# Seven block products instead of eight in the last blocks of four jobs, and operand halves issued two per step there

## The chip, the cores and the metric

The kernel runs on one core of a Trainium2 chip. The metric is the device time of one execution in microseconds (us). The engines are named as in the profile: PE (TensorE, matmuls), PEld (its weight loads), DVE (VectorE), ACT (ScalarE), POOL (GpSimd) and SP (SyncE, which issues nearly all DMAs here).

## What is computed

One layer of a streaming encoder in fp32 on 2048 tokens of width 1024: token mixing (sliding-window attention beside a gated recurrence), cross-attention into 256 memory tokens, and a SwiGLU feed-forward, each inside RMS norms. The change lies in the feed-forward:

```
u = rms_norm(h, g_ffn_pre[l])
y = (jax.nn.silu(u @ w_gate[l]) * (u @ w_up[l])) @ w_down[l]
h = h + rms_norm(y, g_ffn_post[l])
```

`w_gate` and `w_up` are 1024 x 2816, `w_down` is 2816 x 1024.

## The kernel before

**Products.** A fp32 operand is split into a rounded part and a remainder (hi and lo, `split2`, line 982: hi by a copy on ACT or POOL, lo by a subtraction on DVE), and each product of 128 x 128 by 128 x 512 is three matmuls: hi hi, hi lo, lo hi (`products`, lines 1122 to 1124).

**Blocks.** From the output projection on, all large products go through `phases` (line 1210). A block is a 2 x 2 scheme: the moving operand T (resident, four quarters of nk x 128 rows by 512 columns) times the stationary operand S (streamed, 256 columns). There are two ways to do a block:

- seven products (kind "s", `seven`, line 1126), by combinations of the quarters. It uses the resident operands 1, 5, 6, 3, 7, 2, 4 in that order; 1, 2 and 3 are plain quarters, 5, 6, 7 and 4 are sums and differences of them. The stream gives 7 splits and 4 combinations on DVE (`streamed`, line 1063), three first parts are copied off PSUM by ACT (line 1137), and three of the four outputs are additions on DVE.
- eight products (kind "p", `eight`, line 1166) by the plain quarters 1, 2, 8, 3, with 4 stream splits and no combination. It takes two products in each of its 4 steps; a seven-product block takes one in each of its 7.

**Jobs.** `jobs` (line 1411) lists them in order: output projection, scores, values, the feed-forward half 0 and half 1 (each 1024 tokens of u as T, 22 blocks that alternate gate and up over the hidden columns), and three chunks of the down product (8 blocks each, w_down as T; nk is 3 in the first, 4 in the others). `kinds` (line 1423) makes every block "s" and the last one of a job "p"; the very last block of the last job is set back to "s" by hand. In the output projection the first block is "p" too.

**Resident operands.** Seven buffers hold T operands (four of one pool, three of another, line 1227). A queue of operands, in order of first use, is fed by `half` (line 1262): when the buffer with the earliest last use is free at the present step, half an operand is taken up: its DMA into a "row" buffer (nine of them) is issued by SP, and its split into hi and lo is put on a list, due two steps later. `split` (line 1253) takes one due entry off that list, an ACT copy and a DVE subtraction for each half. Sums for 5, 6, 7 and 4 have been made earlier and lie in DRAM (`u0_s`, `u_s`, `d_s`). If an operand is asked for and not there yet, `Ready` (line 1288) issues what is missing at once.

**The order.** The main loop (lines 1331 to 1360) goes through the steps. After a step's matmuls are traced it makes the stream operands two steps ahead (`upto`), advances the work that trails a block (`after`), and calls `split` and `half` once in a step of a seven-product block, twice in a step of an eight-product block. A split that is due is queued behind the step's last ACT and DVE instructions (`behind`, line 1048). The tile framework's scheduler then orders the traced instructions of each engine; after that, each engine runs its list in order.

**Outputs near the change.** Gate blocks end in a Silu on ACT, up blocks in a product on DVE and a store of the hidden rows by SP (line 78). A down block's rows are stored to `y2_d` (shown as `y_d`); from the second chunk on, POOL first adds what is there by an accumulating DMA (line 1500), and SP's store waits for it.

Of the kernel before, what the change touches and what calls it, by code (L numbers as in the profile page):

```python
# [25 lines left out]
NFF = DFF // P  # L26
# [3 lines left out]
NT = T // P  # L30
# [18 lines left out]
class Layer:  # L49
# [89 lines left out]
    def split(self, raw, hi, lo, engine="P"):  # L139

        self.split2(raw, hi, lo, engine)
# [52 lines left out]
    def mix(self):  # L194
        tc, I = self.tc, self.I
        kw = dict(reuse_waits="tile")
        with contextlib.ExitStack() as left:
# [43 lines left out]
            with tc.tile_pool(name="xp", bufs=1, side="right", **kw) as self.xp:  # L241
                fold = self.fold_cross()
                for _ in range(2):
                    next(fold)
                for i, _ in enumerate(pairs, 1):
                    for _ in range(2):
                        next(fold)
                    if 2 <= i < 10:
                        next(phases)
                for _ in fold:  # L250
                    pass
# [199 lines left out]
    def in_first(self):  # L451
# [83 lines left out]
        phases = self.phases([(lambda i, j, a, n: raw[i, j][:, a:a + n, :], 4, blocks, None, {})], T)  # L535
        PE, ACT, DVE, POOL = (getattr(mybir.EngineType, e) for e in ("PE", "Activation", "DVE", "Pool"))
        next(phases)
        self.turns("h", 36)
        x_loads(1, (0, 1))
# [6 lines left out]
        with self.queued(self.traced(POOL), self.traced(DVE)):  # L546
            next(phases)
# [623 lines left out]
    def plain(self, S, T, nk, out, keep, kind):  # L1171
# [36 lines left out]
        yield  # L1208

    def phases(self, jobs, first, prologue=None):  # L1210


# [18 lines left out]
        if first:  # L1231
            for i, p in enumerate(first):
                k = (0, p, False)
# [5 lines left out]
        def fetch(n, tile):  # L1239
            def get(i, j, a, c):  # L1240
                t = tile().rearrange("p (k d) -> p k d", d=512)[:, :c]
                if j is None:
                    self.load(t.rearrange("p k d -> p (k d)"), jobs[n][3][self.CHAIN.index(i), :, a * 512:(a + c) * 512])
                else:
                    jobs[n][0](t, i, j, a, c)
                return t

            return jobs[n][0] if first else get

        def lag(k):  # L1250
            return 2 if k[1] in self.BLOCK or jobs[k[0]][3] is not None else 0

        def split(g):

            if pending and pending[0][0] <= g:
                _, k, f = pending.pop(0)
                f()
                left[k] -= 1
                return True
            return False  # L1260

        def half(g, tile):

            if current[0] is None:
                if not queue:
                    return False
                free = min(slots, key=lambda s: s[1])
                if free[1] > g:
                    return False
                n, p, _ = k = queue.pop(0)  # L1270
                slots.remove(free)
                slots.append((free[0], uses[k][-1], free[2]))
                self._n += 1
                dst = (self.big if free[0] == "A" else self.tb).tile(
                    [P, 2, 4, 512], F32R, tag="big" if free[0] == "A" else "T", name=f"T_{self._n}",
                    bufs=4 if free[0] == "A" else 3)[:, :, :jobs[n][1]]
                T[k] = dst
                left[k] = 2
                current[:] = [(k, self.resident(fetch(n, tile), jobs[n][1], p, dst, keep[n], jobs[n][3] is not None)), 0]
            k, f = current[0]  # L1280
            pending.append((g + lag(k), k, next(f)))
            current[1] += 1
            if current[1] == 2:
                next(f, None)
                current[0] = None
            return True
# [13 lines left out]
        blocks = [b for job in jobs for b in job[2]]  # L1300
        streams, ready, made = [], [], [0]

        def stream(at):
            if at < len(blocks):
                streams.append(blocks[at][1](blocks[at][0]))
                next(streams[-1])

        def upto(count):
            while made[0] < count:
                s = next(streams[0], None)  # L1310
                if s is None:
                    streams.pop(0)
                    continue
                ready.append(s)
                made[0] += 1
# [12 lines left out]
        g = 0  # L1328
        at = 0
        self.last = {}  # L1330
        for _, nk, bl, _, beside in jobs:
            for i, (kind, _, out, follow, addend) in enumerate(bl):
                stream(at + 1)
                after += [f() for f in beside.get(i, ())]
                run = (self.seven(ready, Ready(), nk, out, addend) if kind == "s" else
                       self.eight(ready, Ready(), nk, out) if kind == "p" else
                       self.plain(ready, Ready(), nk, out, addend, kind))
                for q in range(len(self.STEPS[kind])):
                    for _ in range(1 if g or not first else 3):
                        next(run)  # L1340
                        if first and g < 3:
                            yield
                    self.mark()
                    upto(need[g + 2])
                    if first and g == 1:
                        yield
                    for _ in range(1 if kind == "s" else 2):
                        for f in list(after):
                            if next(f, after) is after:
                                after.remove(f)  # L1350
                        if pending and lag(pending[0][1]):
                            with self.behind():
                                split(g)
                        else:
                            split(g)
                        if not first or g > 1:
                            half(g, self.row_tile)
                    g += 1
                after.append(follow())
                at += 1  # L1360
        for f in after:
            for _ in f:
# [48 lines left out]
    def jobs(self):  # L1411
        I = self.I

        def weights(src, r0, nk):
            return lambda t, i, j, k0, n: self.load(
                t, src[r0 + (i * nk + k0) * P:r0 + (i * nk + k0 + n) * P, j * 512:(j + 1) * 512]
                .rearrange("(k p) d -> p k d", p=P))

        def ffn_u(b):
            return lambda t, i, j, k0, n: self.load(  # L1420
                t, self.u_d[4 * i + k0:4 * i + k0 + n, :, b * TB + j * 512:b * TB + (j + 1) * 512]
                .rearrange("k p t -> p k t"))

        def kinds(blocks, n=0):
            return [("p" if i < n or i == len(blocks) - 1 else "s",) + b for i, b in enumerate(blocks)]

        def sums(name, src, nk, other=None):
            return self.sums(name, src, nk, self.extra_tile, other or self.gain_tile)

        def in_turn(*what):  # L1430
            return lambda: itertools.chain.from_iterable(w() for w in what)

        qk, vo = weights(self.qk_d, 0, 4), weights(self.vo_d, 0, 4)
        down = [(weights(I["w_down"], f0 * P, nk), f0, nk) for f0, nk in ((0, 3), (6, 4), (14, 4))]
        qk_s, vo_s = sums("qk_s", qk, 4, self.row_tile), sums("vo_s", vo, 4)
        u_s = sums("u_s", ffn_u(1), 4)
        self.u0_s = self.tc.dram_tile([4, P, 4 * 512], F32, name="u0_s")
        d_s = [sums(f"d_s{c}", src, nk) for c, (src, _, nk) in enumerate(down)]
        jobs = [(self.w_out, 4, kinds([self.mixed_block(n) for n in range(0, NT, 2)], 1), self.out_sums, {1: [qk_s[1]]}),
                (qk, 4, kinds([self.score_block(n) for n in range(0, NT, 2)]), qk_s[0], {1: [vo_s[1]]}),  # L1440
                (vo, 4, kinds([self.value_block(n) for n in range(0, NT, 2)]), vo_s[0], {})]
        for b in range(NB):
            beside = {2: [in_turn(*(d[1] for d in d_s))]} if b else {4: [u_s[1]]}
            jobs.append((ffn_u(b), 4, kinds([blk for f in range(0, NFF, 2) for blk in self.hidden_blocks(b, f)]),
                         u_s[0] if b else self.u0_s, beside))
        for c, (src, f0, nk) in enumerate(down):
            jobs.append((src, nk, kinds([self.down_block(c, f0, nk, n) for n in range(0, NT, 2)]), d_s[c][0], {}))
        k, s, o, f, a = jobs[-1][2][-1]
        jobs[-1][2][-1] = ("s", s, o, f, a)

        return jobs

# [302 lines left out]
```

## Time and profile before

| | |
|---|---|
| time, median of 3 runs | 2589.82 us (2588.64 to 2592.41) |
| span of the profiled execution | 2585.7 us |
| median less that span | 4.1 us |
| busy: PE, PEld, DVE, ACT, POOL | 99%, 83%, 68%, 49%, 17% |
| matmuls and transposes on PE | 12371 |
| DMA | 506.03 MB, mean 196 GB/s |

Only the span is given for the profiled execution; what lies around it is taken to be the 4.1 us between it and the median. A row of the groups names the line, the engine, the operation, what it writes and reads with the shapes, how often, the busy time and the mean of one, and after the bar the engine's idle time just before these instructions with what ended it. In the windows view each engine's busy time and number of instructions stand for a stretch of time, with the granted PE clock, the busy share of the DMA engines and their rate. In the timeline a row gives start, length, engine, line, operation and how many were merged. T is a resident operand, S a stream operand, `psm` a PSUM bank, `sraw` the raw stream, `row` a row buffer, `part` a first part copied off PSUM.

### The profile page before, as it was taken

The page shows a single profiled execution, that of the slowest core. Times are in us where ns is not written, and L with a number is a line of the kernel's source. Part 1 is how long each engine was busy: PE and PEld are TensorE (multiplying, and loading weights), DVE is VectorE, ACT ScalarE, POOL GpSimd, SP SyncE. Part 2 cuts the span into 40 slices and gives each one's busy share as a digit, 9 for nine tenths or more (in the row PEclk, how much of TensorE's full clock was granted, in tenths as well). Part 3 has the DMA queues.
Part 4 walks back from the last instruction along what each step waited for, and adds up shares of the span by engine and source line. Part 5 has one row for each costly group of instructions (what it writes and reads, how often), then busy time and mean ns, then how long its engine had stood idle before and what let it go on. Part 6 is the DMA issues. An engine that isn't in the chain of part 4 may idle for free.

```text
span 2585.7 us, 34998 instructions
## 1 busy us (share of the span) xinstructions
PE 2548.3 (99%) x12371; PEld 2135.9 (83%) x12371; DVE 1747.9 (68%) x2759; ACT 1261.0 (49%) x2633; POOL 428.4 (17%) x612
## 2 busy tenths in 40 slices
PE   9999999999999999999999999999999999999998
PEld 8888888888988778888878888888888888888886
DVE  7785588986557778788876655576566556564656
ACT  5563466665555566465563333353333334443543
POOL 5231334321302232222300000000000000000022
PEclk9999999999999999999999999999999999999999
DMA  6445655855888886666963622253565444566888
GB/s 188 147 163 179 198 168 152 253 185 167 258 290 281 296 287 210 205 222 210 327 233 115 203 97 75 98 203 124 177 205 194 146 146 139 208 201 186 262 213 218
DMA packets 363663, 506.03 MB, mean 196 GB/s; under 512 B 20960, under 2 KB 249312, under 8 KB 363488
## 3 DMA queue, kind: packets, MB, share of 16 engines
q1 hardware_dynamic: 357440, 481.77, 56.5%
q0 software_dynamic: 6048, 22.02, 4.7%
q8 instruction: 97, 1.59, 0.2%
q14 instruction: 78, 0.64, 0.1%
HBM read 337.00 MB, written 166.72 MB: 195 GB/s over the span
## 4 chain that ended last, share of the span: by engine, by line
PE 83%; DMA 7%; DVE 4%; ACT 3%; issue 2%; POOL 1%; SPq 0%; DVEq 0%; POOLq 0%; ACTq 0%
PE psm L1122 23%; PE psm L1124 23%; PE psm L1123 22%; PE psg L156 2%; PE psg L157 2%; PE psg L158 2%; PE pss L1374 1%; DMA row<-y_d 1%; DMA raw<-in_wo_x_dram 1%; DMA u_d<-row 1%; DMA h1t_d<-row 1%; DMA row<-h_d 1%; ACT junk L1471 1%; ACT T L985 0%; PE pss L837 0%
## 5 line engine op out<-in xcount | busy, mean ns | idle before, releaser
L1122 PE MATMUL psm<-T,S 128*128 128x512 f32 x2695 | 1043.8, 391 | 11.0 <-ACT part L1137 6.5
L1123 PE MATMUL psm<-T,S 128*128 128x512 f32 x2695 | 1049.1, 390 | 2.1 <-DVE T L988 1.9
L1124 PE MATMUL psm<-T,S 128*128 128x512 f32 x2695 | 1038.9, 390 | 3.6 <-DVE S L988 3.6
L1122 PEld LDWEIGHTS psm<-T,S 128*128 128x128 f32 x2695 | 506.2, 188 | 120.3 <-ACT part L1137 7.0
L1124 PEld LDWEIGHTS psm<-T,S 128*128 128x128 f32 x2695 | 506.2, 188 | 110.4 <-DVE S L988 5.3
L1123 PEld LDWEIGHTS psm<-T,S 128*128 128x128 f32 x2695 | 506.5, 188 | 107.5 <-DVE T L988 4.1
L985 ACT ACTIVATE S<-sum 128x512 fp32r<-128x512 f32 (+1 forms) x314 | 188.7, 619 | 359.6 <-PE psm L1124 267.8
L988 DVE TENSOR_TENSOR S<-sraw,S 128x512 fp32r<-128x512 f32 (+1 forms) x319 | 217.0, 687 | 215.9 <-ACT S L985 201.8
L988 DVE TENSOR_TENSOR S<-sum,S 128x512 fp32r<-128x512 f32 (+1 forms) x372 | 249.7, 681 | 47.0 <-ACT S L985 31.8
L1137 ACT ACTIVATE part<-psm 128x512 f32<-128x512 f32 x273 | 161.7, 597 | 242.8 <-PE psm L1124 221.5
L985 ACT ACTIVATE S<-sraw 128x512 fp32r<-128x512 f32 (+1 forms) x272 | 167.4, 617 | 111.2 <-PE psm L1124 99.3
L1500 POOL DMA_DIRECT2D row<-y_d x28 | 25.7, 919 | 1111.4 <-DVE row L1686 1036.5
L988 DVE TENSOR_TENSOR T<-row,T 128x1024 fp32r<-128x1024 f32 (+1 forms) x120 | 141.3, 1192 | 60.9 <-ACT T L985 60.4
L1471 ACT ACTIVATE junk<-row 128x512 f32<-128x512 f32 x160 | 99.7, 625 | 60.5 <-DVE row L1493 30.0
L157 PE MATMUL psg<-u,whi 128*128 128x512 f32 x320 | 127.8, 399 | 0.0
L158 PE MATMUL psg<-u,wlo 128*128 128x512 f32 x320 | 127.1, 397 | 0.0
L156 PE MATMUL psg<-u,whi 128*128 128x512 f32 x320 | 127.1, 397 | 0.0
L985 ACT ACTIVATE T<-row 128x1024 fp32r<-128x1024 f32 x120 | 119.9, 1028 | 10.5 <-DMA row<-qk_s 3.5
L987 POOL TENSOR_SCALAR S<-sum 128x512 fp32r<-128x512 f32 x58 | 53.4, 921 | 294.6 <-PE psm L1124 237.2
L1637 DVE TENSOR_TENSOR row<-psm,part 128x512 f32<-128x512 f32 x66 | 43.7, 687 | 61.4 <-PE psm L1124 61.3
L1646 DVE TENSOR_TENSOR part<-psm,part 128x512 f32<-128x512 f32 x60 | 39.7, 687 | 62.4 <-PE psm L1124 62.2
L812 ACT ACTIVATE S<-S,w_mn 128x256 f32<-128x256 f32 (+1 forms) x128 | 63.1, 495 | 28.6 <-DVE w_mn L808 28.3
(363 smaller groups left out, 3679.1 us busy)
## 6 DMA issues: line engine op xcount, KB each, us to landing
sraw<-in_w_gate_dram SPq DMA_DIRECT2D x44, 512.0 KB, 3.7
sraw<-in_w_up_dram SPq DMA_DIRECT2D x44, 512.0 KB, 3.7
hid_d<-row SPq DMA_DIRECT2D x44, 512.0 KB, 2.7
h_d<-row SPq DMA_DIRECT2D x32, 512.0 KB, 4.8
y_d<-row SPq DMA_DIRECT2D x32, 512.0 KB, 3.3
sraw<-hid_d SPq DMA_DIRECT2D x32, 512.0 KB, 5.1
row<-y_d POOLq DMA_DIRECT2D x28, 512.0 KB, 7.1
sraw<-in_w_in_dram SPq DMA_DIRECT2D x44, 256.0 KB, 3.5
```

Of the source, the lines that this page charges most:

```text
L156: nc.tensor.matmul(ps, ah, bh, start=(i == 0), stop=False)
L157: nc.tensor.matmul(ps, ah, bl, start=False, stop=False)
L158: nc.tensor.matmul(ps, al, bh, start=False, stop=(i == n - 1))
L812: nc.scalar.activation(s[:, r, o:], s[:, r, o:], AF.Exp, bias=mn[:, i:i + 1], scale=-1.0, accum_out=den[:, i:i + 1])
L985: self.nc.scalar.activation(hi, raw, AF.Copy)
L987: self.nc.gpsimd.tensor_scalar(hi, raw, 1.0, 1.0, ALU.mult, ALU.mult)
L988: self.nc.vector.tensor_tensor(lo, raw, f32(hi), ALU.subtract)
L1122: nc.tensor.matmul(ps, s[:, 0, k, :], t[:, 0, k, :], start=st, stop=False, **kw)
L1123: nc.tensor.matmul(ps, s[:, 0, k, :], t[:, 1, k, :], start=False, stop=False, **kw)
L1124: nc.tensor.matmul(ps, s[:, 1, k, :], t[:, 0, k, :], start=False, stop=sp, **kw)
L1137: nc.scalar.activation(t, ps, AF.Copy)
L1471: self.nc.scalar.activation(junk, a, AF.Square, scale=float(D) ** -0.5, accum_out=to)
```

## The change

The last block of the two feed-forward halves and of the first two down chunks becomes a seven-product block. In that block two splits may be taken per step and, after its first, fourth and seventh step, a second half; in the block after it, two splits per step. The other jobs (output projection, scores, values) keep their eight-product last block.

```
+        fresh = False
         for _, nk, bl, _, beside in jobs:
             for i, (kind, _, out, follow, addend) in enumerate(bl):
...
+                change = kind == "s" and i == len(bl) - 1
                 for q in range(len(self.STEPS[kind])):
...
                     for _ in range(1 if kind == "s" else 2):
...
                         if not first or g > 1:
                             half(g, self.row_tile)
+                    if change or kind == "s" and fresh:
+                        split(g)
+                        if change and q in (0, 3, 6):
+                            half(g, self.row_tile)
                     g += 1
                 after.append(follow())
+                fresh = change
                 at += 1
...
-        def kinds(blocks, n=0):
-            return [("p" if i < n or i == len(blocks) - 1 else "s",) + b for i, b in enumerate(blocks)]
+        def kinds(blocks, n=0, last="p"):
+            return [("p" if i < n else last if i == len(blocks) - 1 else "s",) + b for i, b in enumerate(blocks)]
...
-            jobs.append((ffn_u(b), 4, kinds([blk for f in range(0, NFF, 2) for blk in self.hidden_blocks(b, f)]),
+            jobs.append((ffn_u(b), 4, kinds([blk for f in range(0, NFF, 2) for blk in self.hidden_blocks(b, f)], 0, "s"),
                          u_s[0] if b else self.u0_s, beside))
         for c, (src, f0, nk) in enumerate(down):
-            jobs.append((src, nk, kinds([self.down_block(c, f0, nk, n) for n in range(0, NT, 2)]), d_s[c][0], {}))
-        k, s, o, f, a = jobs[-1][2][-1]
-        jobs[-1][2][-1] = ("s", s, o, f, a)
+            jobs.append((src, nk, kinds([self.down_block(c, f0, nk, n) for n in range(0, NT, 2)], 0, "s"), d_s[c][0], {}))
```

The extra `split` is not put behind the step's last instructions, as the one in the loop above it is.

## Prediction

> **What bounds the kernel now.** I read the page first: the busy times, then the chain that ended last.
>
> ```profile
> span 2585.7 us, 34998 instructions
> ...
> PE 2548.3 (99%) x12371; PEld 2135.9 (83%) x12371; DVE 1747.9 (68%) x2759; ACT 1261.0 (49%) x2633; POOL 428.4 (17%) x612
> ...
> PE 83%; DMA 7%; DVE 4%; ACT 3%; issue 2%; POOL 1%; SPq 0%; DVEq 0%; POOLq 0%; ACTq 0%
> ```
>
> PE is busy nearly all the time and makes up most of the chain, so a removed matmul is worth something only if PE finds its next operand ready. The stretch that the change touches is then read by groups of instructions (PE alone, the idle time before each group in the last column), and as one window.
>
> ```profile
> L1123 PE MATMUL psm<-T,S 128*128 128x512 f32 x1702 | 661.1, 389 | 0.0
> L1124 PE MATMUL psm<-T,S 128*128 128x512 f32 x1702 | 654.4, 389 | 0.0
> L1122 PE MATMUL psm<-T,S 128*128 128x512 f32 x1702 | 653.5, 389 | 0.0
> ...
> core 0: us, PE busy (x) PEld busy (x) DVE busy (x) ACT busy (x) POOL busy (x), PEclk, DMA share, GB/s
> 1342.00:2499.00 1157.00, 1157.00 (x5106) 958.01 (x5106) 692.44 (x1013) 462.61 (x796) 26.28 (x35) 1.00 0.52 165
> ```
>
> From 1342 to 2499 us PE never waits: 5106 matmuls in 1157.00 us, one every 1157.00 / 5106 = 0.2266 us (389 ns is the length of one, overlapped). All four changes that the diff touches lie in it. So PE alone bounds this stretch, and I have to ask two things: how many matmuls go, and what waits appear in their place.
>
> **The change part by part.** An eight-product block runs 8 x nk x 3 matmuls, a seven-product block 7 x nk x 3. Three of the four blocks have nk 4 (12 fewer each), the first down chunk has nk 3 (9 fewer): 45, which is also the difference of the two built programs' PE lists. 45 x 0.2266 = **10.2 us** off PE if nothing waits. That is certain as work.
>
> The other lists of the built programs differ by 32 more on DVE, 10 more on ACT, 8 fewer on SP, none on POOL. Per block DVE gains 3 stream splits, 4 combinations and 3 additions of outputs and loses the two splits of operand 8; SP loses that operand's two loads. PE's third PSUM bank per block comes from a pool of six; I cost it at nothing, since seven-product blocks run back to back without a wait in the rows above (if a bank were late, PE would wait one DVE output, 0.6 us below).
>
> The extra calls of split and half do no work of their own; they move operand loads and splits. Before, the eight-product block needed operands 1, 2, 8, 3 only, so the buffers of 5, 6, 7 and 4 were free a block early. Now all seven are used to the end, the next job's operand p can be written only after the last block's product p, and it is needed seven products later. Fourteen halves, each one ACT copy and one DVE subtraction, must pass in about two blocks. That is the price to work out. DVE and ACT at the present changes (first and second, third and fourth row are one change each, the last two rows are the changes of the down chunks):
>
> ```profile
> 1692.00:1730.00 38.00, 38.00 (x169) 31.46 (x168) 26.04 (x33) 19.68 (x27) 0.00 (x0) 1.00 0.73 262
> 1730.00:1768.00 38.00, 38.00 (x170) 31.45 (x169) 28.85 (x40) 20.14 (x31) 0.00 (x0) 1.00 0.28 88
> 2114.00:2150.00 36.00, 36.00 (x161) 29.80 (x160) 21.61 (x32) 16.62 (x27) 0.00 (x0) 1.00 0.62 219
> 2150.00:2164.00 14.00, 14.00 (x64) 11.58 (x63) 12.53 (x19) 9.24 (x16) 0.00 (x0) 1.00 0.26 85
> 2240.00:2275.00 35.00, 35.00 (x156) 28.97 (x155) 25.65 (x34) 21.25 (x34) 0.00 (x0) 1.00 0.93 328
> 2403.00:2441.00 38.00, 38.00 (x170) 31.45 (x169) 26.20 (x31) 23.49 (x34) 2.90 (x4) 1.00 0.93 301
> ```
>
> DVE is the fuller of the two, 60 to 90% busy. Its operations overlap, so I take spacings, start to start, from its timeline, and ACT's from the ACT timeline below them:
>
> ```profile
> 1698.96 0.69 DVE L1097 TENSOR_TENSOR sum<-sraw,sraw 128x512 f32<-128x512 f32 x1 [1.49 <-DMA sraw<-in_w_gate_dram]
> 1699.68 0.69 DVE L1097 TENSOR_TENSOR sum<-sum,sraw 128x512 f32<-128x512 f32 x1
> ...
> 1703.77 1.28 DVE L1637 TENSOR_TENSOR row<-psm,part 128x512 f32<-128x512 f32 x2
> 1704.97 1.28 DVE L988 TENSOR_TENSOR S<-sraw,S 128x512 fp32r<-128x512 f32 x2
> 1706.17 1.22 DVE L988 TENSOR_TENSOR T<-row,T 128x1024 fp32r<-128x1024 f32 x1
> ...
> 1712.85 2.36 DVE L988 TENSOR_TENSOR T<-row,T 128x1024 fp32r<-128x1024 f32 x2 [4.05 <-ACT T L985]
> 1715.12 0.68 DVE L1648 TENSOR_TENSOR row<-psm,row 128x512 f32<-128x512 f32 x1
> ...
> 2162.11 1.02 DVE L988 TENSOR_TENSOR S<-sum,S 128x384 fp32r<-128x384 f32 x2
> 2163.05 0.68 DVE L1686 TENSOR_TENSOR row<-psm,part 128x512 f32<-128x512 f32 x1
> 2163.65 0.68 DVE L988 TENSOR_TENSOR T<-row,T 128x512 fp32r<-128x512 f32 x1
> 2164.25 0.55 DVE L1097 TENSOR_TENSOR sum<-sraw 128x384 f32<-128x384 f32 x1
> ...
> 1711.76 2.95 ACT L985 ACTIVATE T<-row 128x1024 fp32r<-128x1024 f32 x3
> 1714.61 0.62 ACT L985 ACTIVATE S<-sraw 128x512 fp32r<-128x512 f32 x1
> 1715.13 4.04 ACT L985 ACTIVATE T<-row 128x1024 fp32r<-128x1024 f32 x4
> ```
>
> 512 columns on DVE: (1706.17 - 1703.77) / 4 = 0.60 us (0.72 where it reads the one before it). 1024: (1715.12 - 1712.85) / 2 = 1.14. 384: (2163.05 - 2162.11) / 2 = 0.47. ACT: 0.95 for 1024, 0.52 for 512, so 14 copies take 13.3 us and ACT stays under three quarters full.
>
> DVE's work in the last block and the block after it, against PE's time for the two (84 x 0.2266 = 19.0 us, or 63 x 0.2266 = 14.3 us at nk 3):
> half 0 to half 1: 18 x 0.60 (up: 7 splits, 4 combinations, 7 for the outputs) + 14 x 0.60 (gate: 7, 4, 3) + 14 x 1.14 = 35.2 of 38.1 us.
> half 1 to the first chunk: 10.8 + (11 x 0.47 + 3 x 0.60) + 7 x (1.14 + 0.60) = 30.0 of 33.3.
> first to second chunk: 7.0 + 8.4 + 16.0 = 31.4 of 33.3.
> second to third: 8.4 + 8.4 + 16.0 = 32.8 of 38.1.
> So it fits, at 86 to 94% full, with 1.9 to 5.3 us to spare and about six dependent combinations at 0.12 more (0.7 us). Whether each operand is in time is a question of order. In the built program PE does not run the products one by one: at each change it places matmuls that need only the rounded half (L1122, after ACT) ahead, and takes products 1 and 5 of the following block while it waits for 7, 2 and 4. I therefore walked the DVE list from the last block's first matmul (0 us), each operation at the latest of the one before it, its ACT copy and, for an output, PE's end. Half 0 to half 1: every low part is there before its first matmul, the nearest (7) at 31.6 us against 34.0. Half 1 to the first chunk: nearest is 7, at 30.2 against 30.4. Second to third chunk: 7 at 33.2 against 33.1. First to second chunk is the tightest, and there the loads count too:
>
> ```profile
> row<-d_s SPq DMA_DIRECT2D x20, 512.0 KB, 8.2
> ...
> row<-in_w_down_dram SPq DMA_DIRECT2D x18, 512.0 KB, 5.7
> ...
> row<-y_d POOLq DMA_DIRECT2D x28, 512.0 KB, 7.1
> ```
>
> SP asks for 6 only behind the store of the block before (ACT's last copy, near 7 us); 7.5 + 8.2 lands about 16 us, its low part is ready at 18.6 against 20.9. That holds DVE back 2 us, so 3 comes at 25.6 against 24.7, and 7 at 30.3 against 29.5 once PE has waited 0.9: about 1.7 us lost. A walk of this kind leaves out the small gaps between engines, and the trace of before shows no change this full, so I bound a change's cost: below by 0 (no wait in the rows above, and no reason for a gain beyond the matmuls), above by the one change where PE did wait, from the value block into half 0:
>
> ```profile
> 1249.00:1342.00 93.00, 88.47 (x409) 71.94 (x408) 77.41 (x91) 62.86 (x126) 18.42 (x26) 0.98 0.84 283
> ...
> PE psm L1123 <- DVE T L988: 1.0, 2, 0.8
> ```
>
> There DVE was 77.41 / 93.00 = 83% full and PE idle 93.00 - 88.47 = 4.5 us. I take 1.7 us for the tightest change and 0.5 for each other, nearer to the lower end because the other six windows, as full as 90%, show no wait: 3.2 us in all.
>
> The DMA engines are the second cover. The third change already runs them at 0.93 and 328 GB/s. From the last block's start SP has some 22 transfers of 512 KB queued there: 0.524 / 0.328 = 1.6 us each, 35 us, where PE has 33.3 us; the halves of 4 stand last, at about 32 us, and PE wants them at 38, so this is hidden with 4 us to spare after copy and split. The Trainium skill, "HBM Reference", Specifications, says that a core that streams alone measures about 425 GB/s. By that it would be 1.2 us each (an estimate from that page) and the DMA would be out of the question; this trace's fullest windows show 328 and 301 at 0.93, and bear the slower figure out.
>
> Sum: -10.2 + 3.2 = -7.0 us on the profiled execution, 2585.7 to 2578.7. The median of the runs shown is 2589.82, 4.1 us above that span; I carry the difference over: 2589.8 - 7.0 = **2582.8 us**.
>
> **The rivals.** *VectorE takes it back.* If the changes cost 2.5 us each (a little over half of the upper bound, 4.5), the sum is -10.2 + 10.0: 2589.6, no difference. For it: 94% full, an in-order queue in which one late ACT copy holds the outputs behind it, and the 4.5 us above. Against it: PE's order leaves 7, 2 and 4 for last, and the later changes of the same form passed without a wait.
>
> *SP's queue holds the operands (slower).* Behind the second chunk's blocks the store of a row waits for POOL's accumulating transfer, and loads stand behind it on SP. POOL's issue, and SP's next store:
>
> ```profile
> 2407.34 0.86 POOL L1500 DMA_DIRECT2D row<-y_d  x1 [10.84 <-DMA row<-d_s]
> ...
> 2415.33 0.34 SPq L78 DMA_DIRECT2D y_d<-row  x1
> ```
>
> That is 8.0 us. At the fourth change the loads of 6, 3, 7 and 2 stand behind two such stores, at the third behind a plain one. My walk has 6 land by 17 us and used from 26; less 3 us for copy, split and queue, 6 us are to spare. If a hold is 8 us longer than now at both, and DMA at 0.93 cannot catch up, PE loses the 8 us twice: -10.2 + 16 + 1.0 (the other two changes) = +6.8: 2596.6 us. It decides where the second store of the block before leaves SP later than 15 us into the last block. For it: 0.93 share; against it: two loads fewer per change, and the first four halves are asked for ahead of that store. The Trainium skill, "TensorE: Matmul & The Clock Gate", What's actually happening, adds that after an idle window of about 3.4 us PE runs at half clock until it has been busy as long. By that rule each such wait would cost up to 1.7 us more (an estimate from that page), 2600 us; in this trace the clock fell only to 0.98 in the window with 4.5 us idle, in pieces, and no row here tests it.
>
> *The change does not do what it says* can be left out: the lists show the 45 matmuls gone.
>
> **How the numbers follow.** A measurement of this kernel can tell about 0.2% (5.2 us) from no change. Forecast (up to 5 us of the 10.2 lost): 0.66. VectorE takes back 5 to 15 us: 0.24. Slower by the queue, or by more than 15 us lost: 0.10. So faster 0.66, same 0.24, slower 0.10. Range: the lower end is no wait at all and 1 us of scatter, 2578.5; the upper reaches into the second case, 8.4 us lost, 2588.0, and leaves out some 0.18.
>
> **What would show it.** PE's list: 45 matmuls fewer, spacing still 0.2266. DVE in the two blocks at each change 86 to 94% full. PE's waits between 1342 us and the end: a few on "DVE T", "ACT T" or "DVE S", together near 3 us, most at the change from the first to the second chunk. Wrong would be waits on DMA rows longer than 3 us (the queue), many waits on DVE outputs or S splits (VectorE), or idle PE away from the four changes. Also wrong is a change of PE's spacing, as the whole gain hangs on it.

## Result and profile after

The changed kernel took 2586.34 us (median of 8 executions, 2581.28 to 2591.21), the kernel before, run beside it, 2592.8 us (8 executions, 2588.64 to 2594.0). The ratio is 0.9978, 95% interval 0.9969 to 0.9987: 5.7 us faster (3.4 to 8.0). A second set of runs of the same two kernels gave 0.9964 (0.9951 to 0.9976). That is 9.3 us (6.2 to 12.7), so the gain is clear of zero and its size is not settled by the times. The two traces of the changed kernel, compared below with the one trace of before, show 4.4 and 4.3 us, inside the first interval and under the second. By the traces 5.8 of the 10.2 us of matmuls that were taken out came back.

The page of the changed kernel, same rows as those shown of before:

```profile
span 2584.3 us, 34943 instructions
...
PE 2540.1 (98%) x12326; PEld 2126.7 (82%) x12326; DVE 1762.3 (68%) x2791; ACT 1262.6 (49%) x2643; POOL 427.2 (17%) x612
...
PE 77%; DMA 7%; issue 6%; DVE 4%; ACT 4%; POOL 1%; SPq 1%; POOLq 0%; DVEq 0%; ACTq 0%
```

PE has 45 matmuls fewer (12371 to 12326), DVE 32 operations more, and PE's part of the chain has gone from 83 to 77%: PE now waits in the stretch in which it never waited. The windows are laid over each changed block and the block after it (in the order of the columns as before):

```profile
1709.00:1748.50 39.50, 38.70 (x170) 31.40 (x169) 33.05 (x44) 24.93 (x36) 0.00 (x0) 1.00 0.72 249
2127.00:2161.00 34.00, 34.00 (x151) 28.15 (x150) 26.99 (x43) 22.27 (x38) 0.00 (x0) 1.00 0.66 226
2246.00:2280.00 34.00, 33.81 (x148) 27.32 (x147) 28.54 (x38) 24.95 (x36) 0.00 (x0) 1.00 0.94 338
2393.60:2436.00 42.40, 40.07 (x169) 32.37 (x168) 30.55 (x39) 24.95 (x36) 3.45 (x4) 0.96 0.99 306
```

PE's busy column against the length of the window shows idle time at the first, third and fourth change, none at the second. The fourth stands out in two more columns: the granted clock is 0.96, and the DMA engines are at 0.99. PE's waits by releaser, from 1342 us to the end (line, who released it, us, times, longest):

```profile
PE psm L1122 <- DVE row L1691: 3.2, 2, 2.3
PE psm L1122 <- DVE part L1139: 1.1, 1, 1.1
PE psm L1122 <- ACT part L1137: 0.7, 1, 0.7
PE psm L1122 <- ACT T L985: 0.2, 1, 0.2
```

(L1691 is L1686 of before, an output of a down block; the lines behind the edit have moved by 5.) A PSUM bank is late far more than an operand is, by this view. The timeline around the longest of these waits shows what the bank stood behind:

```profile
2402.88 0.86 POOL L1505 DMA_DIRECT2D row<-y_d  x1 [6.38 <-ACT row L1695]
...
2409.29 0.32 SPq L78 DMA_DIRECT2D y_d<-row  x1
2409.67 1.23 SPq L75 DMA_DIRECT2D row<-d_s  x2
...
2416.57 1.06 ACT L985 ACTIVATE T<-row 128x1024 fp32r<-128x1024 f32 x1 [5.10 <-DMA row<-d_s]
2417.66 1.23 DVE L988 TENSOR_TENSOR T<-row,T 128x1024 fp32r<-128x1024 f32 x1 [4.22 <-ACT T L985]
...
2419.41 0.68 DVE L1691 TENSOR_TENSOR row<-psm,part 128x512 f32<-128x512 f32 x1
...
2420.14 0.50 PE L1122 MATMUL psm<-T,S 128*128 128x512 f32 x1 [2.33 <-DVE row L1691]
```

Read it upwards from PE. PE waits 2.33 us for a bank that DVE has not yet emptied. DVE is not busy: it sat idle 4.22 us for the rounded half of an operand, because the split of operand 6 stands ahead of that output in its list. ACT sat idle 5.10 us for the operand's row. The row was asked for at 2409.67 and took 6.9 us. And SP asked so late because its store of a y2 row stood ahead and waited for POOL's accumulating transfer of 2402.88. So the name in the waits view (DVE) is the last link only; the first is SP's wait for a DMA. The load itself, 6.9 us, was no slower than the 8.2 us that the prediction took for it. The gap has a second cost, seen in windows of 2 us behind it:

```profile
2420.00:2422.00 2.00, 1.86 (x6) 1.51 (x7) 2.00 (x3) 0.74 (x2) 0.00 (x0) 0.73 1.03 344
2422.00:2424.00 2.00, 2.00 (x7) 1.52 (x6) 2.00 (x4) 0.64 (x1) 0.00 (x0) 0.50 1.02 411
2424.00:2426.00 2.00, 2.00 (x10) 1.65 (x9) 0.85 (x2) 1.64 (x3) 0.32 (x1) 0.92 1.04 389
```

The granted clock falls to 0.50 and PE counts as busy all the while; eight matmuls start 0.427 us apart instead of 0.2266, 1.6 us lost that no wait shows.

To compare kernels I add up, at each change, what PE's spacings start to start exceed 0.2266 us (spacings over 0.25 us). For the changed kernel that is 1.34, 0, 0.66 and 4.31 us at the four changes, 6.3 in all, and 2.42 in the last chunk (3.07 before). From the 7000th matmul (counted from 0), which starts before anything the edit touches, to the last one the trace is 4.43 us shorter than that of before: -10.2 + 6.3 - 0.65 = -4.5. The sum closes. (The 7000th matmul itself starts 3.15 us later in the trace of after, 1359.03 against 1355.88 us; in the experiments, alike up to there, it starts anywhere from 1355.5 to 1364.4. That is scatter of the execution, and why I compare from there on.)

### The profile page after: what moved, and what is told of

It is laid out like the page before. It is cut to its first block, busy times and chain, and to the rows that moved or that the text cites. A ratio compares the mean times of both kernels' runs of the same rounds, so it can differ in the third digit from the quotient of the medians.

```text
span 2584.3 us, 34943 instructions
## 1 busy us (share of the span) xinstructions
PE 2540.1 (98%) x12326; PEld 2126.7 (82%) x12326; DVE 1762.3 (68%) x2791; ACT 1262.6 (49%) x2643; POOL 427.2 (17%) x612
## 4 chain that ended last, share of the span: by engine, by line
PE 77%; DMA 7%; issue 6%; DVE 4%; ACT 4%; POOL 1%; SPq 1%; POOLq 0%; DVEq 0%; ACTq 0%
PE psm L1122 21%; PE psm L1123 21%; PE psm L1124 21%; PE psg L158 2%; PE psg L156 2%; PE psg L157 2%; PE pss L1381 1%; DMA row<-y_d 1%; ACT T L985 1%; DMA y_d<-sg 1%; ACT junk L1476 1%; DMA x<-in_w_out_dram 1%; DMA h1t_d<-row 1%; DMA raw<-in_wo_x_dram 0%; SPq L75 0%
## 5 line engine op out<-in xcount | busy, mean ns | idle before, releaser
L985 ACT ACTIVATE S<-sum 128x512 fp32r<-128x512 f32 (+1 forms) x330 | 198.6, 618 | 363.2 <-PE psm L1124 269.3
L988 DVE TENSOR_TENSOR S<-sum,S 128x512 fp32r<-128x512 f32 (+1 forms) x388 | 260.3, 679 | 45.9 <-ACT S L985 30.3
L1137 ACT ACTIVATE part<-psm 128x512 f32<-128x512 f32 x285 | 168.7, 596 | 239.8 <-PE psm L1124 219.7
L1505 POOL DMA_DIRECT2D row<-y_d x28 | 25.5, 911 | 1111.1 <-DMA sraw<-hid_d 955.0
L988 DVE TENSOR_TENSOR T<-row,T 128x1024 fp32r<-128x1024 f32 (+1 forms) x112 | 132.2, 1192 | 43.9 <-ACT T L985 43.5
L985 ACT ACTIVATE T<-row 128x1024 fp32r<-128x1024 f32 (+1 forms) x112 | 113.9, 1031 | 23.6 <-DMA row<-d_s 8.5
L1642 DVE TENSOR_TENSOR row<-psm,part 128x512 f32<-128x512 f32 x66 | 43.7, 687 | 68.2 <-PE psm L1124 68.2
L1691 DVE TENSOR_TENSOR row<-psm,part 128x512 f32<-128x512 f32 x72 | 49.0, 688 | 52.8 <-PE psm L1124 52.8
```

The lines of the kernel that those rows point to most:

```text
L985: self.nc.scalar.activation(hi, raw, AF.Copy)
L988: self.nc.vector.tensor_tensor(lo, raw, f32(hi), ALU.subtract)
L1137: nc.scalar.activation(t, ps, AF.Copy)
L1691: nc.vector.tensor_tensor(d, a, b, ALU.add)
```

## Experiments

All are edits of the changed kernel unless the text says otherwise. In the table the losses are in us, as defined above; "pace" is the time from the 7000th to the last matmul against that of before, and ratios are to the kernel before beside it, with 95% intervals.

| kernel | 1st | 2nd | 3rd | 4th | last chunk | pace | ratio |
|---|---|---|---|---|---|---|---|
| before | 0 | 0 | 0 | 0 | 3.07 | 0 | 1 |
| after | 1.34 | 0 | 0.66 | 4.31 | 2.42 | -4.43 | 0.9978 (0.9969 to 0.9987) |
| after again | 1.34 | 0 | 0.94 | 3.99 | 2.42 | -4.32 | 0.9964 (0.9951 to 0.9976) |
| store by POOL | 1.34 | 0 | 0.82 | 4.05 | 1.24 | -5.55 | 0.9969 (0.9957 to 0.9981) |
| feed-forward only | 1.34 | 0 | 0 | 0 | 3.31 | -3.72 | 0.9983 (0.9972 to 0.9994) |
| down chunks only | 0 | 0 | 1.07 | 2.14 | 1.56 | -2.92 | 0.9974 (0.9963 to 0.9986) |
| no extra halves | 9.03 | 5.05 | 7.93 | 11.61 | 4.47 | +25.34 | 1.0085 (1.0063 to 1.0106) |
| all steps | 0.28 | 0 | 1.16 | 2.45 | 2.43 | -6.79 | 0.9967 (0.9955 to 0.9979) |
| all steps, store by POOL | 0.28 | 0 | 1.37 | 0.58 | 4.10 | -6.79 | 0.9961 (0.9948 to 0.9975) |
| no y2 rows at the fourth | 1.34 | 0 | 1.73 | 0.11 | 4.89 | -4.76 | 0.9962 (0.9948 to 0.9976) |
| sums on POOL | 1.11 | 0 | 0.92 | 4.08 | 1.74 | -5.24 | 0.9968 (0.9957 to 0.9979) |
| all steps at nk 4, store by POOL | 0.28 | 0 | 3.57 | 0.23 | 5.29 | -3.69 | 0.9973 (0.9962 to 0.9983) |
| all steps, store by POOL, no adds in the last chunk | 0.28 | 0 | 0.23 | 0.14 | 1.12 | -11.52 | 0.9963 (0.9949 to 0.9978) |

A single ratio has an interval of some 6 us, as wide as the whole effect: but for the one above 1, the ratios do not tell these versions apart. The verdicts below rest on the losses in the traces, one trace for each version; the two traces of the changed kernel agree within 0.3 us at each change, and no other version was traced twice.

**Is it the store behind POOL's addition?** The y2 rows of the second chunk are stored by POOL itself, so that SP's list has no wait for an addition.

```diff
-                    self.store(self.y2_d[(n + i) * P:(n + i + 1) * P, :], y[i])
+                    (self.nc.gpsimd.dma_start if c else self.store)(self.y2_d[(n + i) * P:(n + i + 1) * P, :], y[i])
```

> Edit: the rows of the second down chunk are stored to y2_d by POOL's queue, behind its own accumulating transfer, so that SP's queue no longer waits for that transfer. Theory (SP's queue holds the loads of operand 6 at the fourth change, its split then holds an output on DVE that PE's last product of the old job needs): no PE wait over 0.5 us at the fourth change, granted clock 1.00 there, the waits of the first and third change (1.3 and 0.7 us) as they were; -10.2 + 2.0 = about -8 us, ratio 0.997. Rival (DVE is too full at every change, whoever issues the stores): PE still idle 2 us or more at the fourth change, ratio 0.998 as with the change itself.

The loss at the fourth change stayed at 4.05 us, so the expectation failed; but it is another loss. Operand 6 was asked for 3 us earlier in the block (not at once: SP now stood behind the load of a stream tile, which waits for its raw buffer), and the gap between starts 20 us into the block fell from 2.71 to 0.50 us. A new gap of 2.19 us came at 27 us, where PE waited for a first part that ACT copied only behind late operands, and the clock fell again behind it. SP's issues, and under them PE's waits for such copies (in all, times, longest; the 0.7 us beside the longest belongs to the first change):

```profile
2396.74 0.90 SPq L75 DMA_DIRECT2D row<-d_s  x2
2409.21 0.37 SPq L75 DMA_DIRECT2D sraw<-hid_d  x1
2409.69 1.82 SPq L75 DMA_DIRECT2D row<-d_s  x2
...
PE psm L1122 <- ACT part L1137: 2.5, 2, 1.8
```

The loads of operand 7 left SP at 20.1 us into the block, after a wait of 6.0 us for the store of a y2 row to land: the rows of y2 and those of the operands share the nine row buffers, so a store that is late holds the loads even when another queue issues it.

**One half of the change alone.** The down chunks, or the feed-forward halves, keep their eight-product blocks:

```diff
-            jobs.append((src, nk, kinds([self.down_block(c, f0, nk, n) for n in range(0, NT, 2)], 0, "s"), d_s[c][0], {}))
+            jobs.append((src, nk, kinds([self.down_block(c, f0, nk, n) for n in range(0, NT, 2)], 0, "s" if c == 2 else "p"), d_s[c][0], {}))
```

> Edit: only the two feed-forward halves end in a seven-product block; the first two down chunks keep their eight-product last block. 24 matmuls fewer than before: -5.4 us of PE work. Theory (waits belong to the single changes: 1.3 us at the first, none at the second): -4.1 us, ratio 0.9984, no wait at the third and fourth change. Rival (each change gives back the same 1.6 us): -2.2 us, ratio 0.9991.

```diff
-            jobs.append((ffn_u(b), 4, kinds([blk for f in range(0, NFF, 2) for blk in self.hidden_blocks(b, f)], 0, "s"),
+            jobs.append((ffn_u(b), 4, kinds([blk for f in range(0, NFF, 2) for blk in self.hidden_blocks(b, f)]),
```

> Edit: only the first two down chunks end in a seven-product block; the feed-forward halves keep their eight-product last block. 21 matmuls fewer: -4.8 us of PE work. Theory (0.7 us of waits at the third change, 4.4 us with the slowed clock at the fourth): +0.3 us, ratio 1.000. Rival (each change gives back the same 1.6 us): -1.6 us, ratio 0.9994.

The loss of 1.34 us at the first change is the same with or without the down chunks, and waits at the third and fourth come only where these are changed. Of the feed-forward's 5.4 us (24 matmuls) 3.7 arrive, near the 4.1 expected. Of the down chunks' 4.8 us (21) 2.9 arrive, which neither theory had (0.3 us slower, or 1.6 faster): the fourth change loses 2.14 us there and not 4.4. Most of the difference is the clock, which stayed at full speed (the longest gap was 1.55 us).

**The extra split and half left out.**

```diff
-                    if change or kind == "s" and fresh:
-                        split(g)
-                        if change and q in (0, 3, 6):
-                            half(g, self.row_tile)
```

> Edit: the extra calls of split and half at the changes are taken out; the four last blocks still have seven products. 45 matmuls fewer, -10.2 us. Theory (operand halves that come later are what PE waits for): one half per step brings the last operand's halves some three steps (8 us) later, so waits of 2 to 4 us at each of the four changes, -10.2 + 12 = about +2 us, ratio 1.0005. Rival (DVE's total work decides, not the order of the halves): the same waits as with the change, ratio 0.998.

22 us slower than before. All four changes lose, 33.6 us together, and now PE waits for operands themselves:

```profile
PE psm L1122 <- ACT T L985: 11.7, 7, 4.8
PE psm L1123 <- DVE T L988: 11.0, 11, 1.9
```

I had the direction, but took it for an effect of a few us; against the changed kernel it is 28 us by the two ratios and 30 us by the traces. A seven-product block by itself would have made this kernel slower; taking the operands in earlier is what lets the removed matmuls count.

**Both halves of every operand at once.** The extra half is taken at every step of the changed block.

```diff
-                        if change and q in (0, 3, 6):
+                        if change:
```

> Edit: in the changed last blocks the extra half is taken at every step, not only at the first, fourth and seventh, so both halves of an operand are asked for together. Theory: the 1.34 us at the first change are a matter of order (the tail of product 5 stands directly ahead of product 3 in the same bank, so 3 waits for ACT's copy of the bank); in this build it no longer does, so that wait falls below 0.3 us, the third below 0.3; the fourth change is bound by its DMA and keeps 2 to 5 us. Ratio to before about 0.998. Rival (DVE is too full there): DVE's work is the same, so the waits of the first and third change stay at 2 us or more in sum.

The first change falls from 1.34 to 0.28 us, as expected from the order of PE's list: in the list of the changed kernel the last matmuls of product 5 stand directly ahead of product 3, both in one PSUM bank, so 3 waits for ACT's copy of the bank (0.7 us in the waits view above); in this build they do not. The third did not fall (1.16 where under 0.3 was expected). The fourth fell to 2.45, but only because the clock stayed at full speed: the gaps alone cost 2.45 us, against 2.7 in the changed kernel.

**The same, with the store by POOL.** Both edits together.

> Edit: the halves at every step as in the run beside it, and the second chunk's stores issued by POOL behind its additions, so that SP's queue never waits for them. Theory (the fourth change is bound by the rate of its DMAs, not by SP's wait): 2 to 5 us still lost at the fourth change, under 0.6 us in sum at the others; ratio 0.996 to 0.998. Rival (SP's wait for the addition holds the operands, and asking for halves together is what it lacked): under 0.7 us at the fourth change, ratio 0.9955.

0.58 us at the fourth change, as the rival had it: the theory that the rate of the DMAs alone sets it fell too, since the DMA engines are as full as ever.

```profile
2400.00:2420.00 20.00, 20.00 (x90) 16.57 (x89) 15.26 (x20) 13.17 (x19) 2.88 (x4) 1.00 1.03 328
2420.00:2440.00 20.00, 19.98 (x87) 15.95 (x87) 17.14 (x22) 13.48 (x20) 2.04 (x4) 1.00 0.98 293
```

**Eight transfers fewer at the fourth change.** The last two blocks of the second chunk neither add nor store their rows: this part of the sum is left out of the output.

```diff
             for i in range(0 if late else 2):
+                if c == 1 and n >= NT - 4:
+                    continue
```

> Edit: the last two blocks of the second chunk neither add nor store their rows (that part of the sum is left out), so eight transfers of 512 KB fewer lie around the fourth change. Theory (DMA is full there): the wait of 4.3 us at the fourth change falls below 0.7 us and the clock stays at 1.00; first change 1.3 and third 0.7 us as before; ratio about 0.996. Rival (DVE is too full there): the work on DVE is the same, so 2 us or more stay at the fourth change.

The fourth change loses 0.11 us, with the clock at 1.00 and DMA at 0.65 and 0.52. DVE is 94% busy in the second window (18.88 of 20.00 us), so a full DVE does not decide. The run asks for operand 6 as late as the first experiment did, but for operand 7 much earlier (below): with the transfers it also takes away the hold on SP's queue and on the row buffers, so by itself it does not show that the rate of the DMA engines is what counts.

```profile
2400.00:2420.00 20.00, 20.00 (x90) 16.57 (x89) 13.93 (x19) 12.08 (x17) 0.00 (x0) 1.00 0.65 233
2420.00:2440.00 20.00, 20.00 (x90) 16.22 (x89) 18.88 (x24) 13.56 (x20) 0.00 (x0) 1.00 0.52 188
```

**DVE relieved.** The combinations of the stream in the changed blocks and the blocks after them, 32 in all, go to POOL.

```diff
-            nc.vector.tensor_tensor(t, a, b, op)
+            (nc.gpsimd if light else nc.vector).tensor_tensor(t, a, b, op)
```

> Edit: the combinations of the stream (8 additions in all) of each changed last block and of the block after it are made by POOL instead of DVE, which takes some 4.8 us off DVE at each change. Rival (DVE is too full): the waits at all four changes fall below 0.5 us each, ratio about 0.9955. Theory (order at the first change, DMA at the fourth): the first change keeps 1 us or more, the fourth 2 us or more; ratio 0.997 to 0.999, and worse if POOL is slow enough for PE to wait for stream operands.

1.11, 0.92 and 4.08 us are still lost. DVE has eight sums of 0.69 us less around each change and PE waits as before. The relief is small in the windows of the two blocks themselves, 0.3 to 1.7 us of DVE's busy time, since half of the sums lie ahead of them; together with the run before, in which DVE was 94% busy for 20 us and PE did not wait, it speaks against DVE's fullness as the cause.

**The changed kernel again, and one more version.** It takes all steps in the blocks with nk 4, the first, fourth and seventh in the first chunk, and the store by POOL.

> The changed kernel once more, on the chip and beside the runs of before that the next run shares, so that the two can be set side by side. Expected: ratio to before 0.9978, inside 0.9969 to 0.9987, and the same waits (1.34, 0, 0.66 and 4.3 us at the four changes, within 0.5 us each). If the waits at the third and fourth change differ by more, they hang on the execution and not on the program.

> Edit: the second chunk's stores issued by POOL, and the extra half taken at every step of the changed last blocks with nk 4, at the first, fourth and seventh step in the first chunk. Theory (a wait comes where an operand is asked for late while the DMA engines are full; asking early or moving less each cures it, and at the third change asking for all halves at once had cost 0.7 us): first change below 0.4 us, second 0, third 0.6 to 0.9, fourth below 1, in sum under 2.3 against 6.3 in the changed kernel; ratio 0.9955 to 0.9965, 0.0015 below the changed kernel beside it. Rival (the DMA rate alone sets the fourth change and the 0.6 us of the other version were luck): 2 us or more at the fourth change, ratio 0.997 to 0.998.

The waits of the changed kernel came back within 0.3 us each, so at the first, second and fourth change I take them for the program's; its ratio, 0.9964, lies just under the expected 0.9969 to 0.9987. In the other version the fourth change is cured again (0.23 us, DMA share 1.03 and 0.98), but the sum I expected is wrong: 3.57 us at the third change and 5.29 in the last chunk. At the third change the loss moves from 0.2 to 3.6 us between versions, between some that are the same program up to that place (0.66, 0.94 and 1.73; 1.37 and 0.23). I leave its cause open; the DMA engines are at 0.94 there.

The fourth change can now be taken apart, in all versions that change it and keep the extra halves. Times are in us from the start of the changed block (756 matmuls ahead of the last one): when SP issued the first load of operands 6 and 7, which lie ready-made in DRAM, and when ACT began to copy them; then PE's losses, divided into gaps up to 25 us into the block, later gaps, and matmuls at half clock.

| kernel | 6 asked | 6 copied | gaps to 25 us | 7 asked | 7 copied | later gaps | half clock |
|---|---|---|---|---|---|---|---|
| after | 12.6 | 19.5 | 2.60 | 16.5 | 29.7 | 0.11 | 1.60 |
| after again | 12.8 | 19.2 | 2.31 | 16.7 | 29.4 | 0.07 | 1.60 |
| sums on POOL | 13.2 | 19.3 | 2.36 | 17.8 | 29.5 | 0.11 | 1.61 |
| store by POOL | 9.3 | 17.3 | 0.38 | 20.1 | 28.0 | 2.07 | 1.60 |
| down chunks only | 11.9 | 17.5 | 0.59 | 15.7 | 27.6 | 1.54 | 0 |
| all steps | -2.9 | 10.7 | 0 | 16.0 | 27.1 | 2.45 | 0 |
| no y2 rows at the fourth | 9.2 | 15.7 | 0 | 11.7 | 25.5 | 0.11 | 0 |
| all steps, store by POOL | -2.8 | 10.6 | 0 | 12.1 | 25.2 | 0.58 | 0 |
| all steps at nk 4, store by POOL | -2.6 | 10.3 | 0 | 12.0 | 24.9 | 0.23 | 0 |
| all steps, store by POOL, no adds in the last chunk | -2.5 | 10.3 | 0 | 11.9 | 24.8 | 0.14 | 0 |

The first gap follows operand 6 alone: there is none where ACT copies it by 15.7 us, and from about 17.0 us on PE waits as long as the copy is late (0.50 us from start to start at 17.3, 2.71 at 19.5). Where 6 is in time or nearly so, a later gap follows operand 7: 1.5 us or more where it is copied after 27 us, at most 0.58 where it is copied by 25.5. Each single edit cures one operand and leaves the other. The store by POOL brings 6 forward, but 7 waits for a row buffer; all steps ask for 6 early, but 7 stands on SP behind two stores. With both edits 7 is asked for at 12 us, and little is lost though the DMA engines are full.

How much of the lateness is late asking and how much is slow landing stays open. The halves of operand 7 took 9.3 and 8.2 us to land in the run with the eight transfers fewer, 9.3 and 11.5 in "all steps, store by POOL"; but no run asks for 7 late while the engines have room.

**Where the rest goes.** Three versions that cure the fourth change lose more in the last chunk, 4.10, 4.89 and 5.29, against 2.42 in the changed kernel and 3.07 before. The timeline of "all steps, store by POOL" there:

```profile
2501.78 0.86 POOL L1505 DMA_DIRECT2D row<-y_d  x1 [1.11 <-ACT row L1695]
...
2512.87 0.63 ACT L1476 ACTIVATE junk<-row 128x512 f32<-128x512 f32 x1 [2.34 <-DMA row<-y_d]
...
2515.02 0.73 POOL L1491 TENSOR_TENSOR q_r<-q_w,mhalf 128x2 f32<-128x2 f32 x1
2515.78 1.29 DVE L1733 SCALAR_TENSOR_TENSOR row<-row,q_r,g 128x1024 f32<-128x1024 f32 x1 [7.32 <-POOL q_r L1491]
```

POOL adds the earlier chunks' rows at 2501.78; they land 11 us later, ACT squares them, POOL makes the scale, and DVE, whose next instruction is the normalisation, has sat idle for 7.32 us with the outputs of the block behind it. The windows there hold the DMA share at 0.99 and 0.97. Before the change DVE stood idle there in the same way, up to 6.92 us; in the changed kernel it was 3.68 us at most. The last run, made from this version, takes the accumulating transfers of the last chunk away (the rows of the first two chunks are left out of most of its sums):

```diff
-                if c:
+                if c == 1:
                     self.add(y[i], self.y2_d, n + i)
```

> Edit: the version with all halves at every step and POOL's stores, and besides no accumulating transfer in the last chunk (the rows of the first two chunks are left out of the sum there; 12 transfers of 512 KB fewer). Theory (what the fourth change no longer loses, the last chunk takes: DVE's normalisation of a row waits 6 to 8 us for the accumulated row, with the DMA engines full): the waits between 2500 and 2545 us, 2.98 us in that version's profile, fall below 0.5 us, and from the index 7000 of the matmuls to the end the kernel is 8.5 to 10.5 us shorter than before, against 6.8 with the adds; ratio 0.9950 to 0.9960. Rival (the waits of the last chunk come from DVE's outputs, whatever the DMA does): 2 us or more stay there, ratio 0.996 to 0.9975.

```profile
2500.00:2520.00 20.00, 20.00 (x90) 16.57 (x89) 12.05 (x17) 9.56 (x20) 2.92 (x5) 1.00 0.82 234
2520.00:2545.00 25.00, 25.00 (x112) 20.71 (x111) 15.54 (x23) 11.24 (x25) 3.36 (x8) 1.00 0.62 182
...
2507.22 1.28 DVE L1733 SCALAR_TENSOR_TENSOR row<-row,q_r,g 128x1024 f32<-128x1024 f32 x1 [3.09 <-POOL q_r L1491]
```

PE does not wait between 2500 and 2545 us any more, DVE's idle time before the normalisation is 3.09 instead of 7.32, and the pace is -11.52 us, a little more than expected: -10.2 + 0.65 at the changes - 1.95 in the last chunk. So the waits of the last chunk do come from the accumulated rows. Without them the removed matmuls are worth 9.6 of their 10.2 us, and the 2 us that before lost there come on top. The ratio, 0.9963 (0.9949 to 0.9978), would be 10 us, just short of what was expected; its interval, 6 to 13 us, holds the 11.5 of the trace. No version that computes the whole sum was shown to be faster than the changed kernel: the best, 0.9961 (0.9948 to 0.9975), overlaps with its two ratios.

## Why the prediction came out as it did

The predicted 2582.8 us lies 3.5 us under the measured median; the range, 2578.5 to 2588.0, holds it, and faster by over 0.2% was the likeliest case. The gain was forecast at 7.0 us and is 5.7 (3.4 to 8.0) against the kernel before beside it, which itself was 3 us slower than the 2589.82 that the forecast starts from. The sign was right because the first term was. The second term was half of what the traces show, 3.2 against 6.3 us, and stood at the wrong changes. That the time still fell into the range is in part luck: the range is 9.5 us wide, and two of the four changes cost less than forecast while the other two cost more. The sign that was to show it came out otherwise too: PE's waits were to be few on operands, about 3 us, most at the change from the first to the second chunk; the waits view has 0.2 us on an operand and 5.0 on PSUM banks, the longest wait, 2.3 us, at the fourth change.

- **"45 x 0.2266 = 10.2 us off PE if nothing waits."** Right. The matmuls are gone, and when most of their waits go as well (last run), the pace shows 9.6 of the 10.2.
- **DVE "at 86 to 94% full", "so it fits".** It does, and with more room than was forecast: the windows above show DVE busy 84, 79, 84 and 72% of the two blocks. "VectorE takes it back" has the run with the sums on POOL and the one with DVE 94% busy and next to no loss against it, and its 2.5 us a change came up at one change only. Its words "an in-order queue in which one late ACT copy holds the outputs behind it" are what the trace shows there, but that copy is late by a DMA.
- **"1.7 us for the tightest change and 0.5 for each other", 3.2 in all.** This failed. Measured: 1.34, 0, 0.66 and 4.31, 6.3 in all. The change called tightest, first to second chunk, lost 0.7 to 0.9. The first change's 1.34 us is the order of two products in one bank, which the walk of DVE's list could not see, as it gave PE no banks.
- **"My walk has 6 land by 17 us and used from 26".** This is the step that fails, at the fourth change. Operand 6 was asked for at 12.6 us and landed at 19.5, its second half at 21.1. Neither landing took longer than the 8.2 us that the walk used at the third change; the request was late. And its use at 26 us did not matter: its split stands in DVE's list ahead of an output, so its lateness reaches PE by a PSUM bank, from 17.0 us on and long before PE wants the operand. Of the 6 us to spare there were none. The row buffers, which the y2 rows share with the operands, were in no step of the walk, and the loads were counted against the rate of the DMA engines at the third change only ("hidden with 4 us to spare"); at the fourth POOL's additions and the y2 stores come on top, and the engines run at 0.99 for 42 us.
- **"SP's queue holds the operands".** Its mechanism is there and its price was not. The store left SP 12.3 us into the block, short of the 15 us from which the rival was to decide, and the fourth change lost 4 us, not 8. Taking the store away from SP removed the gap that it had caused and uncovered another, so that the sum did not move (4.05); with the halves asked for together it cured the place (0.58).
- **The clock.** The Trainium skill, "TensorE: Matmul & The Clock Gate", What's actually happening, puts the half clock behind an idle window of about 3.4 us. Here the gap was 2.7 us start to start, 2.33 us by PE's wait, and the clock did fall to 0.50. The extra cost weighed in the prediction, up to 1.7 us per wait, was right in size (1.6), but it came with a shorter wait than that rule asks for; it is part of the 4.31. The trace of before could have told: the 0.98 that the prediction read as hardly a fall is the mean of 93 us, and holds 3.41 us at 0.50, from 1306.64 us on, right behind a gap of 2.32 us.
- **The last chunk** was in no step. The trace of before has 3.07 us of lost time there, and I took that stretch as not touched by the edit. It is touched: the changed kernel loses 0.65 us less there, and three versions that come out of the fourth change with little loss lose 1.0 to 2.2 us more there than before, in waits that go away with the accumulating transfers (last run).

## What to carry to other kernels

When a block's operands are needed in less time, follow each load from the moment at which it can be asked for: what stands ahead of it on its queue, which buffer it needs and who still holds that buffer, and only then how long it takes to land beside the other transfers of its stretch. Follow a late operand through the in-order list of the engine that prepares it, since it stops the outputs behind it, and so PE, by a bank and not by the operand. Look again after each cure, since a cured wait can uncover the next one with the same sum. And before a gain on PE is booked, look for the next place at which work comes at a pace that PE does not set, here the last chunk's accumulating transfers: time saved ahead of it was partly given back there.

## What the runs showed of the hardware

- PE's clock changes in steps of 3.41 us, and how much of one step PE works decides, not the length of a gap. In each of the thirteen traces all changes of the granted clock lie on a grid of 3.413 us, and within the program the half clock lasts one step or two. From 1342 us to the last matmul, with 0.2266 us counted for each matmul, the half clock followed all seven full-clock steps in which PE worked less than 0.40 of the time (0.09 to 0.39) and none of the others (0.44 and more). So a gap of 2.19 us between starts halved the clock where it lay in one step (share 0.39, the store by POOL), as did 2.42 and 2.71 us (0.32 and 0.24, the two runs of the changed kernel); one of 2.78 us, which lay across two steps (0.52 and 0.69, the run without the extra halves), did not.
- "Full" DMA engines moved very different amounts: at a share of 1.02 to 1.04, between 344 and 411 GB/s in the windows of 2 us above, at 0.98 and 0.99 some 293 and 306. A rate alone does not tell whether the engines are full.
- POOL took 1.3 to 1.6 us for an addition in fp32 (the medians of its four groups of eight, six of 128 x 512 and two of 128 x 384 in each), DVE 0.69 for 128 x 512.
